# Output projection of a decoder layer: seven products of half-size blocks in place of eight

## The chip, the core and the metric

The kernel runs on one core of a Trainium2 chip. Its work goes to five engines, each with a queue of its own: TensorE (PE in the profile; the loading of stationary operands is shown apart as PEld), VectorE (DVE), ScalarE (ACT), GpSimd (POOL) and SyncE (SP), which issues DMAs. Each engine executes its instructions in the order in which they are written, and waits for other engines by semaphores. The metric is the time of one execution on the device in microseconds; lower is better.

## The reference

One layer on 512 tokens of width 1024, all in float32: a normalised input, one large input projection, two groups of heads (mLSTM and block-sparse attention), and an output projection into the residual. Only the end is changed:

```
y_ml = h_ml.reshape(B, S, ML_WIDTH) * jax.nn.silu(ml_z)     # 512 tokens x 512
y_at = o_at.reshape(B, S, AT_WIDTH) * jax.nn.silu(at_z)     # 512 tokens x 512
y = jnp.concatenate([y_ml, y_at], axis=-1).astype(x.dtype) @ w_out   # w_out 1024 x 1024
return x + y
```

In blocks, with two halves of 256 tokens (1 and 2), the two halves of the contraction (ml and at) and two halves of 512 output columns (0 and 1), each output block is a sum of two products: out(1,c) = y_ml1 B0c + y_at1 B1c, out(2,c) = y_ml2 B0c + y_at2 B1c. These are eight products of blocks, each 256 tokens by 512 by 512 columns.

## The kernel before

**Products.** TensorE multiplies in a rounded float32. To keep the precision, each operand is split into a rounded high part and the remainder (hi and lo), and each product is formed as three matmuls, hi by hi, hi by lo and lo by hi (`mm3`, L343). ScalarE makes the hi (a copy that rounds, CAST), VectorE the lo (the operand less its hi, TENSOR_TENSOR). So a weight piece of 128 x 1024 (two tiles of 128 rows by 512 columns) costs one CAST and one subtraction before it can be used.

**Weights** come in a list of pieces (L202 to L206 add the eight of w_out: `wo0` for columns 0 to 511, `wo1` for the others, four each). `load_w` (DMA at L234, into one of three buffers `raw`) loads a piece ahead of its use, `g_split` (L237) splits it into `whi` and `wlo`, and `need_w` waits for it.

**The order of the work.** Projections are one main stream that is written out in loops. All that runs beside them (splits, evacuations, heads) are small programs, held by `Plan`. After every few matmuls `plan.run()` resumes each program whose estimated time has come, and its instructions are appended to the queues of the engines. The estimates are clocks per engine with a rate and a fixed cost (`Engine`). The order in a queue is thus fixed when the kernel is built; at run time nothing overtakes. Instructions of VectorE, ScalarE and GpSimd are recorded at line L75, matmuls at L173, transposes at L177; the tile names tell them apart.

**Left sides.** `put_y` (L646) writes hi and lo of y for 128 features and all 512 tokens: the four mLSTM heads into buffers `br`, the four attention tiles (made in `ev_z`, L764, with the gate z in `cv0` and `cv1`) into `xh` and `xl`.

**The output stage** (L872 to L889). For the columns 0 to 511, four tiles of 128 tokens run in four PSUM banks at once, first over the mLSTM half of the contraction, then over the attention half. For the other columns the tiles run one by one, and the last one in two halves of 256 columns. `ev_out` (L863) adds the residual, loaded beforehand into `tq` and `tk`, on VectorE and stores the tile by a DMA of SyncE:

```
o = xres[half][t][:, c0:c1]
t_ = dve.tensor_tensor(o, ps[:, :c1 - c0], o, op=ALU.add)
banks.put(t_, ps)
nc.sync.dma_start(out[t * P:(t + 1) * P, half * 512 + c0:half * 512 + c1], o)
```

## Time and profile before

| | us |
|---|---|
| three runs | 310.49, 310.58, 310.62 (median 310.58) |
| the profiled execution, its span | 308.8 |
| median of the runs less that span | 1.8 |
| TensorE busy | 303.2 (98%) |
| VectorE busy | 185.8 (60%) |
| ScalarE busy | 150.2 (49%) |
| GpSimd busy | 58.3 (19%) |

The span reaches from the first to the last record of the profiled execution; the time of a run holds what lies around the records too. The busy times are shares of the whole span. The kernel moves 31.80 MB by DMA. A timeline's start is counted from the beginning of the span; equal instructions that follow each other are drawn together (x3), with the time from the first start to the last end.

### The profile page before, as it was taken

The numbers are of one execution on the slowest core, as the hardware profiler recorded it, in microseconds if no ns is written. First come the engines' busy times: TensorE is split into PE (matmuls) and PEld (weight loads), VectorE is DVE, ScalarE is ACT, GpSimd is POOL, SyncE is SP. The second block draws the span as 40 slices with busy tenths as digits, with TensorE's granted clock in tenths as the row PEclk, the third lists the DMA queues.
The fourth block names the chain that finished last, engine by engine and source line by source line (L and its number), as shares of the span: only waits on it lengthen the run. The fifth ranks groups of instructions, "written<-read, shape, count | busy, mean of one in ns | idle before, by whom it ended". The sixth has DMA issues, their size and how long they took to land.

```text
span 308.8 us, 4284 instructions
## 1 busy us (share of the span) xinstructions
PE 303.2 (98%) x1594; PEld 248.2 (80%) x1594; DVE 185.8 (60%) x395; ACT 150.2 (49%) x271; POOL 58.3 (19%) x94
## 2 busy tenths in 40 slices
PE   7999999999999999999999999999999999999995
PEld 3999888778888868886886888688889978788885
DVE  4892458935456549999627995501568999714111
ACT  3372754314365671775439356899763237420000
POOL 3000164262501800450150005110000060000000
PEclk9999999999999999999999999999999999999999
DMA  7997122141410410132103021400252102832101
GB/s 198 394 412 300 68 69 75 63 137 49 155 70 0 168 39 9 60 128 78 68 2 137 0 83 55 138 0 2 93 176 73 44 24 72 306 135 102 36 34 68
DMA packets 10821, 31.80 MB, mean 103 GB/s; under 512 B 1328, under 2 KB 1584, under 8 KB 10800
## 3 DMA queue, kind: packets, MB, share of 16 engines
q1 hardware_dynamic: 10800, 31.53, 28.8%
q8 instruction: 12, 0.20, 0.3%
q14 instruction: 9, 0.07, 0.1%
HBM read 29.42 MB, written 2.10 MB: 102 GB/s over the span
## 4 chain that ended last, share of the span: by engine, by line
PE 95%; DMA 2%; SPq 1%; DVE 1%; ACT 0%; issue 0%
PE bank L173 89%; PE bank L177 6%; DMA tq<-in_xT_dram 2%; ACT xh L75 0%; DVE wlo L75 0%; SPq L306 0%; DVE xl L75 0%; SPq L234 0%; SPq L232 0%; DVE tk L75 0%; SPq L230 0%; SPq L180 0%
## 5 line engine op out<-in xcount | busy, mean ns | idle before, releaser
L173 PE MATMUL bank<-whi,xh 128*128 128x512 f32 (+2 forms) x260 | 86.4, 367 | 0.7 <-DVE whi L75 0.7
L173 PE MATMUL bank<-wlo,xh 128*128 128x512 f32 (+2 forms) x260 | 85.1, 363 | 0.2 <-DVE wlo L75 0.2
L173 PE MATMUL bank<-whi,xl 128*128 128x512 f32 (+2 forms) x260 | 85.2, 363 | 0.0
L75 DVE TENSOR_TENSOR wlo<-raw,whi 128x1024 fp32r<-128x1024 f32 x39 | 48.0, 1241 | 10.8 <-ACT whi L75 9.2
L173 PEld LDWEIGHTS bank<-whi,xh 128*128 128x128 f32 x260 | 45.1, 188 | 8.7 <-ACT xh L75 1.1
L173 PEld LDWEIGHTS bank<-whi,xl 128*128 128x128 f32 x260 | 45.0, 188 | 8.1
L173 PEld LDWEIGHTS bank<-wlo,xh 128*128 128x128 f32 x260 | 45.1, 188 | 7.9 <-DVE wlo L75 0.6
L75 ACT CAST whi<-raw 128x1024 fp32r<-128x1024 f32 x39 | 40.8, 1048 | 19.8 <-PE bank L173 11.5
L173 PE MATMUL bank<-xh,whi 128*128 128x512 f32 x96 | 40.9, 426 | 0.0
L173 PE MATMUL bank<-xh,wlo 128*128 128x512 f32 x96 | 37.9, 395 | 0.0
L173 PE MATMUL bank<-xl,whi 128*128 128x512 f32 x96 | 37.7, 393 | 0.0
L75 POOL TENSOR_SCALAR b<-b,rec 128x128 f32<-128x128 f32 (+3 forms) x32 | 18.9, 612 | 84.6 <-DVE rec L75 67.1
L75 ACT ACTIVATE br<-bank,sm 64x512 fp32r<-64x512 f32 (+1 forms) x28 | 19.1, 684 | 14.7 <-DVE br L75 9.7
L173 PEld LDWEIGHTS bank<-xh,whi 128*128 128x128 f32 x96 | 18.2, 190 | 4.5 <-issue 2.1
L173 PE MATMUL bank<-whi,br 128*128 128x512 f32 (+1 forms) x72 | 21.4, 370 | 0.0
L173 PEld LDWEIGHTS bank<-xh,wlo 128*128 128x128 f32 x96 | 18.0, 188 | 4.2
L75 ACT ACTIVATE b<-b,mn 128x128 f32<-128x128 f32 (+3 forms) x32 | 17.6, 553 | 7.6 <-DVE mn L75 7.5
L173 PEld LDWEIGHTS bank<-xl,whi 128*128 128x128 f32 x96 | 18.2, 189 | 2.5
L75 DVE SCALAR_TENSOR_TENSOR br<-bank,sm,br 64x512 fp32r<-64x512 f32 (+1 forms) x20 | 15.0, 749 | 5.9 <-ACT br L75 5.6
L75 DVE CUSTOM_DVE_ANT_0 b<-bank,b 128x128 f32<-128x128 f32 (+3 forms) x32 | 14.2, 488 | 5.5 <-PE bank L173 5.4
L173 PEld LDWEIGHTS bank<-whi,br 128*128 128x128 f32 x72 | 13.1, 188 | 2.6
L177 PEld LDWEIGHTS bank<-ident,b 128*128 128x128 f32 (+1 forms) x104 | 12.3, 140 | 3.4 <-issue 0.4
(141 smaller groups left out, 374.1 us busy)
## 6 DMA issues: line engine op xcount, KB each, us to landing
raw<-in_w_in_dram SPq DMA_DIRECT2D x31, 512.0 KB, 3.2
raw<-in_w_out_dram SPq DMA_DIRECT2D x8, 512.0 KB, 3.5
b<-in_w_in_dram SPq DMA_DIRECT2D x3, 520.0 KB, 7.5
tq<-in_xT_dram SPq DMA_DIRECT2D x4, 256.0 KB, 5.4
tk<-in_xT_dram SPq DMA_DIRECT2D x4, 256.0 KB, 7.8
ot<-in_x_dram SPq DMA_DIRECT2D x2, 512.0 KB, 9.1
cv<-in_x_dram SPq DMA_DIRECT2D x2, 512.0 KB, 9.9
tq<-in_x_dram SPq DMA_DIRECT2D x4, 256.0 KB, 5.8
```

What stands on the lines that cost most here:

```text
L75: fn(out, *args, **kw)
L173: nc.tensor.matmul(out_, lhsT=lhsT, rhs=rhs, start=start, stop=stop, skip_group_check=True)
L177: nc.tensor.transpose(out_, in_, idn)
```

## The change

Eight products of blocks are replaced by seven, with an identity of the Strassen family. Its operands are sums and differences of blocks:

| product | left side, 256 tokens x 512 | weights, 512 x 512 |
|---|---|---|
| p5 | y_ml2 | B00 + B01 |
| p1 | xa = y_ml1 - y_at1 | B00 |
| p2 | y_at1 | B00 + B10 |
| p6 | r = y_ml2 - xa | p1's less p7's |
| p3 | c = y_ml1 - y_ml2 | B01 + B11 |
| p7 | e = r - y_at2 | B11 |
| p4 | y_at2 | B10 + B11 |

They are formed in this order. Each has two tiles of 128 tokens, four k-tiles of 128 and three matmuls of 512 columns: 24 matmuls. Products accumulate on each other in three pairs of PSUM banks (`CHAIN`): p5 and then p3 in one pair, p1, p6, p7 and p4 in another, p2 in its own. Between two products of a pair the sum so far is taken out, without the pair being given back, by `ev_prod`. After p5 and p1, ScalarE copies the two banks to SBUF (`vbuf` and `tk`), and a DMA issued by GpSimd adds the tile of x onto the copy (`accum_op`). After p2, p6, p3, p7 and p4, VectorE adds the bank to, or subtracts it from, the output block in SBUF. Where a block is complete it is stored by SyncE; the last tile is no longer halved.

The weights of p5, p2, p3 and p4 are loaded as two pieces onto each other: a plain DMA of SyncE, and 4.5 us later on the plan's clock an accumulating one of GpSimd (`g_load`). Those of p6 are a subtraction on VectorE. Loads go in the order p5, p1, p2, p7, p3, p4, into the three `raw` buffers and others that are free by then (`wraw`, such as `ot` and `sz`).

`put_ml` writes y_ml to `tq` and splits only the tokens of p5; the steps after the gates make xa and its split; `g_combos` makes the other left sides. `x_of(r, c, a)` is a tile of x in DRAM, `store` and `residual` are DMAs of SyncE, and `two`, `of` and `flat2` give views of a tile by k. The main stream then runs over the products:

```diff
@@ -191,29 +191,32 @@
...
+    PRODS = [("p5", [(0, 0), (0, 1)]), ("p1", [(0, 0)]), ("p2", [(0, 0), (1, 0)]), ("p6", []),
+             ("p3", [(0, 1), (1, 1)]), ("p7", [(1, 1)]), ("p4", [(1, 0), (1, 1)])]
+    for name, blocks in PRODS:
+        for u in range(2):
+            pieces.append((name, u, 512, w_out, [(c * 4 + 2 * r + u) * P * 1024 for r, c in blocks]))
     W = {}
+    NREG = sum(p[3] is w_in for p in pieces)
     raws = {}
+    nload, nsplit = [0], [0, sum(p[3] is w_in for p in pieces)]
+    def src_ap(i, b=0):
         _, _, n, src, o = pieces[i]
+        return bass.AP(tensor=src.tensor, offset=src.offset + o[b], ap=[[2 * n, P], [1, 2 * n]])
     def pair(t, n):
         return t[:, :2 * n].rearrange("p (k n) -> p k n", k=2)
@@ -232,19 +237,66 @@
-        raws[i] = pair(dst, n)
+        raws[i] = (dst, pair(dst, n))
     def g_split(i, copy=act.copy, parts=1):
         name, kk, n, _, _ = pieces[i]
-        raw = raws.pop(i)
+        if i >= NREG:
+            yield (0.0, lambda: i in raws and nsplit[1] >= i, False)
+        flat_raw, raw = raws[i][0], raws.pop(i)[1]
...
         W[name, kk] = (hi, lo)
+        if i >= NREG:
+            nsplit[1] = i + 1
+            if name == "p1":
+                wkeep["p1", kk] = flat_raw
+            else:
+                wraw.put(t_, flat_raw)
         load_w()
+    wraw = Bufs(plan, [])
+    nraw, lnext = [0], [0]
+    wkeep = {}
+    at = {(p[0], p[1]): i for i, p in enumerate(pieces)}
+    LOADS = [(n, u) for n in ("p5", "p1", "p2", "p7", "p3", "p4") for u in range(2)]
+    def raw_ok():
+        room = 3 - nraw[0] - max(0, NREG - nsplit[0])
+        return room > 0 or wraw.ok()
+    def raw_get():
+        if wraw.ok():
+            return wraw.get()
+        nraw[0] += 1
+        return wp.tile([P, 1024], F32, name="raw", tag="raw", bufs=3)
+    def g_load(j):
+        name, u = LOADS[j]
+        i = at[name, u]
+        yield (0.0, lambda: lnext[0] == j and raw_ok(), False)
+        dst = raw_get()
+        nc.sync.dma_start(dst, src_ap(i))
+        lnext[0] += 1
+        if len(pieces[i][4]) == 2:
+            yield plan.now + 4500.0
+            nc.gpsimd.dma_start(dst, src_ap(i, 1), accum_op=ALU.add)
+            yield plan.now + 5000.0
+        else:
+            yield plan.now + 5000.0
+        if name == "p7":
+            wkeep["p7", u] = dst
+            yield (0.0, lambda: ("p1", u) in wkeep and ("p6", u) not in wkeep, False)
+            d1 = wkeep["p1", u]
+            t_ = dve.tensor_tensor(d1, d1, dst, op=ALU.subtract)
+            wkeep["p6", u] = d1
+            yield t_
+            raws[at["p6", u]] = (d1, pair(d1, 512))
+        raws[i] = (dst, pair(dst, 512))
@@ -640,19 +692,34 @@
...
+    yml = tq
+    y_at = [cv[f // 2][:, f % 2] for f in range(4)]
+    X = {}
+    H = slice(0, 256), slice(256, 512)
+    def halves(t):
+        return t.rearrange("p (k n) -> p k n", n=256)
+    def put_ml(h, ps, scale, t_=0.0):
+        yield act.activation(yml[:, h], ps, AF.Copy, scale=scale)
+        hi, lo = X["p5"]
+        t_ = act.copy(hi(h), yml[:, h, H[1]])
         yield t_
+        yield dve.tensor_tensor(lo(h), yml[:, h, H[1]], hi(h).bitcast(F32), op=ALU.subtract)
...
@@ -755,7 +822,10 @@
...
         yield plan.now + SLACK
-        for t_ in put_y(h, ps, sm[:, C_MN + h:C_MN + h + 1]):
+        yield when(lambda: have["S"] == MLH)
+        if "p5" not in X:
+            X["p5"] = two([br.get() for _ in range(2)]), two([br.get() for _ in range(2)])
@@ -770,14 +840,70 @@
...
             t_ = dve.tensor_tensor(z, z, ot[:, f], op=ALU.mult)
-            yield when(lambda: have["proj"], t_)
-            for t_ in put_y(4 + f, z, None):
-                yield t_
+            yield when(lambda: have["y"] == MLH, t_)
+            if f == 0:
+                X["xa"] = b5.get()
+                X["p1"] = two([br.get() for _ in range(2)]), two([br.get() for _ in range(2)])
+            xa = halves(X["xa"][:, 0:1024])
+            x1 = xa[:, f]
+            yield dve.tensor_tensor(x1, yml[:, f, H[0]], z[:, H[0]], op=ALU.subtract)
+            hi, lo = X["p1"]
+            yield act.copy(hi(f), x1)
+            yield dve.tensor_tensor(lo(f), x1, hi(f).bitcast(F32), op=ALU.subtract)
+            have["p1"] += 1
         return ev
+    fl = lambda t: t.rearrange("p a n -> p (a n)")
+    def g_combos():
+        yield when(lambda: have["p1"] == 4)
+        wraw.put(plan.now, *[flat(ot)[:, 1024 * u:1024 * u + 1024] for u in range(2)])
+        xa = halves(X["xa"][:, 0:1024])
+        def plain(h, key):
+            for f in range(4):
+                yield act.copy(xh[:, f, H[h]], y_at[f][:, H[h]])
+                yield dve.tensor_tensor(xl[:, f, H[h]], y_at[f][:, H[h]], xh[:, f, H[h]].bitcast(F32), op=ALU.subtract)
+                have[key] += 1
+        for t_ in plain(0, "p2"):
+            yield t_
+        r, c, e = (b5.get()[:, 0:1024] for _ in range(3))
+        rv = halves(r)
+        yield when(lambda: step[0] >= 1)
+        yield dve.tensor_tensor(rv, yml[:, :, H[1]], xa, op=ALU.subtract)
+        yield act.copy(fl(xh[:, 4:6]), r)
+        dve.tensor_tensor(fl(xl[:, 4:6]), r, fl(xh[:, 4:6]).bitcast(F32), op=ALU.subtract)
+        X["p6"] = flat2(xh, 4), flat2(xl, 4)
+        have["p6"] = 4
+        yield when(lambda: step[0] >= 2)
+        yield dve.tensor_tensor(halves(c), yml[:, :, H[0]], yml[:, :, H[1]], op=ALU.subtract)
+        hi, lo = X["p3"] = X["p5"]
+        for k in range(4):
+            act.copy(hi(k), halves(c)[:, k])
+            t_ = dve.tensor_tensor(lo(k), halves(c)[:, k], hi(k).bitcast(F32), op=ALU.subtract)
+        yield t_
+        have["p3"] = 4
+        yield when(lambda: step[0] >= 3)
+        for u in range(2):
+            t_ = dve.tensor_tensor(halves(e)[:, 2 * u:2 * u + 2], rv[:, 2 * u:2 * u + 2], cv[u][:, :, H[1]], op=ALU.subtract)
+        yield t_
+        yield act.copy(fl(xh[:, 6:8]), e)
+        dve.tensor_tensor(fl(xl[:, 6:8]), e, fl(xh[:, 6:8]).bitcast(F32), op=ALU.subtract)
+        X["p7"] = flat2(xh, 6), flat2(xl, 6)
+        have["p7"] = 4
+        yield when(lambda: step[0] >= 4)
+        for t_ in plain(1, "p4"):
+            yield t_
+    step = [0]
...
@@ -841,52 +967,97 @@
...
+    for j in range(len(LOADS)):
+        plan.add(g_load(j), rank=1)
...
+    def ev_prod(ps, a, what, last, c0=0, c1=512):
+        t_ = plan.now
+        for r, c, op, end in what:
+            d = res[r, c, a][:, c0:c1]
+            if op is None:
+                yield act.copy(d, ps)
+                nc.gpsimd.dma_start(d, x_of(r, c, a), accum_op=ALU.add)
+                continue
+            t_ = dve.tensor_tensor(d, d, ps[:, :c1 - c0], op=op)
+            if end:
+                store(r, c, a, c0, c1)
+        if last:
             banks.put(t_, ps)
+        yield t_
+    ADD, SUB = ALU.add, ALU.subtract
+    bank = {}
+    CHAIN = {"p5": ("B", [(1, 1, None, False)]),
+             "p1": ("A", [(0, 0, None, False)]),
+             "p2": ("1", [(0, 0, ADD, True)]),
+             "p6": ("A", [(0, 1, SUB, False)]),
+             "p3": ("B", [(0, 1, ADD, True)]),
+             "p7": ("A", [(1, 1, SUB, True)]),
+             "p4": ("A", [(1, 0, ADD, True)])}
+    ends = {"p2", "p3", "p4"}
+    plan.add(g_combos(), rank=0.5)
+    for name, _ in PRODS:
+        key, what = CHAIN[name]
+        step[0] = [n for n, _ in PRODS].index(name)
+        first = (key, 0) not in bank
+        if first:
+            for a in range(2):
+                bank[key, a] = main_bank()
+        plan.until(lambda: name != "p1" or "p1" in X)
+        left = {"p1": X.get("p1"), "p2": (of(xh, 0), of(xl, 0)), "p4": (of(xh, 1), of(xl, 1))}
+        def part(ps, a, k, c0=0, c1=512, start=False, stop=False):
+            hi, lo = need_w(name, k // 2)
+            plan.until(lambda: name == "p5" or have[name] > k)
+            xs = left.get(name) or X[name]
+            ts = slice(a * P, (a + 1) * P)
+            mm3(ps, xs[0](k)[:, ts], xs[1](k)[:, ts], hi[:, k % 2, c0:c1], lo[:, k % 2, c0:c1], start, stop)
+        if name in ("p7", "p4"):
+            for a in range(2):
+                for k in range(4):
+                    part(bank[key, a], a, k, stop=k == 3)
+                    if a and k % 2 and name == "p7":
+                        split_w()
+                    plan.run()
+                plan.add(ev_prod(bank[key, a], a, what, name in ends), rank=0, ready=plan.now + SLACK)
+            continue
+        for k in range(4):
+            for a in range(2):
+                part(bank[key, a], a, k, start=first and k == 0, stop=k == 3)
                 plan.run()
+            if k % 2:
+                split_w()
+            if name in ("p1", "p2") and k == 0:
+                residual(*((0, 1) if name == "p1" else (1, 0)))
+        for a in range(2):
+            plan.add(ev_prod(bank[key, a], a, what, name in ends), rank=0, ready=plan.now + SLACK)
```

VectorE's queue before, in the output stage: the last split of a left side has just been written, and what follows are the lo parts of weights (`wlo`) and the additions that empty banks.

```order
L75 TENSOR_TENSOR wlo_2376<-raw_2145,whi_2375 128x1024
L75 TENSOR_TENSOR wlo_2379<-raw_2277,whi_2378 128x1024
L75 TENSOR_TENSOR tq_128<-bank5_91,tq_128 128x512
L75 TENSOR_TENSOR tq_128<-bank0_86,tq_128 128x512
L75 TENSOR_TENSOR tq_128<-bank4_90,tq_128 128x512
L75 TENSOR_TENSOR tq_128<-bank6_92,tq_128 128x512
L75 TENSOR_TENSOR wlo_2442<-raw_2299,whi_2441 128x1024
```

VectorE's queue in the changed kernel, from the end of p1 to p6's left side. `cv1` holds y_at, `b5_4` is r, `b5_3` is xa; `wlo_2399` is p2's second weight piece, `wlo_2419` and `wlo_2431` are p6's two, `wlo_2443` is p3's first; `bank3` and `bank7` are p2's banks.

```order
L75 TENSOR_TENSOR xl_112<-cv1_132,xh_111 128x256
L75 TENSOR_TENSOR wlo_2399<-sz_127,whi_2398 128x1024
L75 TENSOR_TENSOR xl_112<-cv1_132,xh_111 128x256
L75 TENSOR_TENSOR wlo_2419<-raw_1985,whi_2418 128x1024
L75 TENSOR_TENSOR b5_4_73<-tq_128,b5_3_72 128x1024
L75 TENSOR_TENSOR wlo_2431<-raw_1981,whi_2430 128x1024
L75 TENSOR_TENSOR tk_129<-tk_129,bank3_89 128x512
L75 TENSOR_TENSOR tk_129<-tk_129,bank7_93 128x512
L75 TENSOR_TENSOR wlo_2443<-ot_133,whi_2442 128x1024
L75 TENSOR_TENSOR xl_112<-b5_4_73,xh_111 128x1024
```

The left side of p6 (the last row) now stands behind two additions that need the end of p2 and behind a weight piece of p3.

Further on in the same queue, from p7's second weight piece (`wlo_2496`) and p4's first (`wlo_2519`) to p7's left side (`b5_0` is e); `bank1` and `bank4` hold p3.

```order
L75 TENSOR_TENSOR wlo_2496<-ot_133,whi_2495 128x1024
L75 TENSOR_TENSOR wlo_2519<-sz_127,whi_2518 128x1024
L75 TENSOR_TENSOR tk_129<-tk_129,bank1_87 128x512
L75 TENSOR_TENSOR tk_129<-tk_129,bank4_90 128x512
L75 TENSOR_TENSOR xl_112<-b5_0_69,xh_111 128x1024
```

Before, nothing but weight pieces and additions stood here; now the left side of the next product stands behind the two additions that need the end of the one before it.

ScalarE's queue before, at its end: the last gate, its hi, and weight pieces.

```order
L75 ACTIVATE cv1_132<-cv1_132 128x512
L75 CAST xh_111<-cv1_132 128x512
L75 CAST whi_2375<-raw_2145 128x1024
L75 CAST whi_2378<-raw_2277 128x1024
L75 CAST whi_2441<-raw_2299 128x1024
L75 CAST whi_2444<-raw_2391 128x1024
```

ScalarE's queue in the changed kernel, from the copies of p1's banks (`bank0`, `bank6`) to p6's left side: `xh` from `cv1` is p2's left side, `whi_2398` p2's second weight piece, `whi_2418` and `whi_2430` p6's two, `whi_2442` p3's first.

```order
L75 COPY tk_129<-bank0_86 128x512
L75 COPY tk_129<-bank6_92 128x512
L75 CAST xh_111<-cv1_132 128x256
L75 CAST whi_2398<-sz_127 128x1024
L75 CAST xh_111<-cv1_132 128x256
L75 CAST whi_2418<-raw_1985 128x1024
L75 CAST whi_2430<-raw_1981 128x1024
L75 CAST whi_2442<-ot_133 128x1024
L75 CAST xh_111<-b5_4_73 128x1024
```

The copies that empty p1's banks, which were no work of ScalarE's before, stand ahead of the second half of p2's operands and of all of p6's.

## Rows read from the trace of the kernel before

**Rows 1.** The page: span, busy times, and shares of the chain that ended last.

```profile
span 308.8 us, 4284 instructions
...
PE 303.2 (98%) x1594; PEld 248.2 (80%) x1594; DVE 185.8 (60%) x395; ACT 150.2 (49%) x271; POOL 58.3 (19%) x94
...
PE 95%; DMA 2%; SPq 1%; DVE 1%; ACT 0%; issue 0%
```

**Rows 2.** Timeline: start, length, engine; first and last matmul of the output stage, last addition.

```profile
260.51 0.39 PE L173 MATMUL bank<-whi,br 128*128 128x512 f32 x1
...
305.04 0.28 PE L173 MATMUL bank<-whi,xl 128*128 128x256 f32 x1
305.35 0.42 DVE L75 TENSOR_TENSOR tk<-bank,tk 128x256 f32<-128x256 f32 x1 [2.42 <-PE bank L173]
```

**Rows 3.** Windows: length, busy PE PEld DVE ACT POOL (count), PE clock, DMA.

```profile
240.00:260.50 20.50, 20.50 (x114) 17.24 (x114) 19.91 (x59) 9.43 (x15) 5.24 (x8) 1.00 0.12 30
260.50:271.60 11.10, 11.10 (x49) 8.87 (x48) 7.63 (x10) 4.49 (x6) 0.00 (x0) 1.00 0.85 309
271.60:282.80 11.20, 11.20 (x50) 9.15 (x49) 2.08 (x3) 1.12 (x2) 0.00 (x0) 1.00 0.23 86
305.40:308.80 3.40, 0.00 (x0) 0.00 (x0) 0.38 (x1) 0.00 (x0) 0.00 (x0) 0.92 0.11 39
```

**Rows 4.** Groups of instructions, 260.4 to 309: count, busy us, mean ns, idle before.

```profile
L173 PE MATMUL bank<-whi,br 128*128 128x512 f32 x56 | 18.3, 396 | 0.0
...
L173 PE MATMUL bank<-whi,br 128*128 128x256 f32 x16 | 3.2, 282 | 0.0
```

**Rows 5.** VectorE from 260: timeline, then groups of its additions.

```profile
260.19 1.22 DVE L75 TENSOR_TENSOR wlo<-raw,whi 128x1024 fp32r<-128x1024 f32 x1
...
262.58 1.89 DVE L75 TENSOR_TENSOR xl<-cv,xh 128x512 fp32r<-128x512 f32 x3
...
266.70 2.36 DVE L75 TENSOR_TENSOR wlo<-raw,whi 128x1024 fp32r<-128x1024 f32 x2 [0.26 <-ACT whi L75]
...
L75 DVE TENSOR_TENSOR tk<-bank,tk 128x512 f32<-128x512 f32 x3 | 2.1, 692 | 12.3 <-PE bank L173 12.3
...
L75 DVE TENSOR_TENSOR tk<-bank,tk 128x256 f32<-128x256 f32 x2 | 0.8, 425 | 4.6 <-PE bank L173 4.6
```

**Rows 6.** ScalarE from 259: timeline, then a group of copies from PSUM.

```profile
259.20 1.65 ACT L75 CAST xh<-cv 128x512 fp32r<-128x512 f32 x3
...
265.11 0.62 ACT L75 CAST xh<-cv 128x512 fp32r<-128x512 f32 x1 [1.77 <-DVE cv L75]
...
265.63 1.99 ACT L75 CAST whi<-raw 128x1024 fp32r<-128x1024 f32 x2
...
270.62 1.05 ACT L75 CAST whi<-raw 128x1024 fp32r<-128x1024 f32 x1 [2.99 <-issue]
...
L75 ACT COPY b<-bank 128x256 f32<-128x256 f32 x8 | 3.0, 375 | 2.9 <-PE bank L177 2.9
```

**Rows 7.** Timeline ahead of the stage: weight loads, a gate, GpSimd's next work.

```profile
221.62 40.15 SPq L234 DMA_DIRECT2D raw<-in_w_out_dram  x7
...
235.86 0.63 ACT L75 ACTIVATE cv<-cv 128x512 f32<-128x512 f32 x1 [2.87 <-DVE cv L75]
...
246.66 0.20 POOL L75 TENSOR_SCALAR mst<-mst 128x4 f32<-128x4 f32 x1 [39.66 <-DVE mst L75]
246.94 1.03 POOL L75 TENSOR_TENSOR mst<-mst,mhalf 128x4 f32<-128x4 f32 x1
```

**Rows 8.** DMA issues with us to landing; SyncE's time per issue, min/median/max ns.

```profile
tk<-in_x_dram SPq DMA_DIRECT2D x4, 256.0 KB, 6.8
...
out_dram<-tk SPq DMA_DIRECT2D x3, 256.0 KB, 2.0
out_dram<-tk SPq DMA_DIRECT2D x2, 128.0 KB, 1.9
...
L868 SPq DMA_DIRECT2D out_dram<-tk x5: 332/332/333, 289.3 to 305.8; - x5
```

More of the change, by code (lines that the diff above doesn't have):

```diff
@@ L199, in hybrid_layer @@
         for kk in range(4):
-            pieces.append((name, kk, n, w_in, off))
+            pieces.append((name, kk, n, w_in, [off]))
             off += P * 2 * n
-    off = 0
-    for half in range(2):
-        for kk in range(4):
-            pieces.append((f"wo{half}", kk, 512, w_out, off))
-            off += P * 2 * 512
+    PRODS = [("p5", [(0, 0), (0, 1)]), ("p1", [(0, 0)]), ("p2", [(0, 0), (1, 0)]), ("p6", []),
[3 more added lines that the diff above has]
+            pieces.append((name, u, 512, w_out, [(c * 4 + 2 * r + u) * P * 1024 for r, c in blocks]))
     xh = sb("xh", [P, KT, S], F32R)
@@ L641, in hybrid_layer, with two, of, flat2 @@
     have["silu"] = have["sig"] = have["gates"] = have["mlive"] = have["W"] = have["S"] = have["y"] = 0
-    yh, yl = {}, {}
-    def put_y(f, src, scale, t_=0.0):
-        hi, lo = (br.get(), br.get()) if f < 4 else (xh[:, f - 4], xl[:, f - 4])
-        if scale is None:
-            yield act.copy(hi, src)
-            t_ = dve.tensor_tensor(lo, src, hi.bitcast(F32), op=ALU.subtract)
-        else:
-            yield act.activation(hi, src, AF.Copy, scale=scale)
-            t_ = dve.scalar_tensor_tensor(lo, src, scale, hi.bitcast(F32), op0=ALU.mult, op1=ALU.subtract)
-        yh[f], yl[f] = hi, lo
-        yield t_
+    yml = tq
[8 more added lines that the diff above has]
+        t_ = act.copy(hi(h), yml[:, h, H[1]])
+        yield t_
+        yield dve.tensor_tensor(lo(h), yml[:, h, H[1]], hi(h).bitcast(F32), op=ALU.subtract)
+    def two(tiles):
+        v = [halves(t) for t in tiles]
+        return lambda k: v[k // 2][:, k % 2]
+    def of(t, h):
+        return lambda k: t[:, k, H[h]]
+    def flat2(t, k0):
+        v = halves(t[:, k0:k0 + 2].rearrange("p a n -> p (a n)"))
+        return lambda k: v[:, k]
     def g_mlstm(h):
@@ L757, in g_mlstm @@
         yield plan.now + SLACK
-        for t_ in put_y(h, ps, sm[:, C_MN + h:C_MN + h + 1]):
+        yield when(lambda: have["S"] == MLH)
+        if "p5" not in X:
+            X["p5"] = two([br.get() for _ in range(2)]), two([br.get() for _ in range(2)])
+        for t_ in put_ml(h, ps, sm[:, C_MN + h:C_MN + h + 1]):
             yield t_
@@ L778, in hybrid_layer @@
+    step = [0]
     have["proj"] = 0
+    for name in ("p1", "p2", "p3", "p4", "p6", "p7"):
+        have[name] = 0
     psz = [[banks.get() for _ in range(2)] for _ in range(NT)]
@@ L846, in hybrid_layer @@
     have["proj"] = 1
-    def out_mm(ps, half, t, k, c0=0, c1=512):
-        plan.until(lambda: k in yh)
-        hi, lo = need_w(f"wo{half}", k // 2)
-        ts = slice(t * P, (t + 1) * P)
-        mm3(ps[:, :c1 - c0], yh[k][:, ts], yl[k][:, ts], hi[:, k % 2, c0:c1], lo[:, k % 2, c0:c1],
-            k == 0, k == KT - 1)
-    xres = []
-    plan.until(lambda: have["y"] == MLH)
-    for half in range(2):
-        r = tk if half else tq
-        for t in range(NT):
-            nc.sync.dma_start(r[:, t], x[t * P:(t + 1) * P, half * 512:half * 512 + 512])
-        xres.append([r[:, t] for t in range(NT)])
@@ L863, in ev_out @@
-    def ev_out(half, t, c0=0, c1=512):
-        def ev(ps):
-            o = xres[half][t][:, c0:c1]
-            t_ = dve.tensor_tensor(o, ps[:, :c1 - c0], o, op=ALU.add)
-            banks.put(t_, ps)
-            nc.sync.dma_start(out[t * P:(t + 1) * P, half * 512 + c0:half * 512 + c1], o)
-            yield t_
-        return ev
-    ps4 = [main_bank() for _ in range(NT)]
-    for ks in ((0, 1, 2, 3), (4, 5, 6, 7)):
-        for t in range(NT):
-            for k in ks:
-                out_mm(ps4[t], 0, t, k)
-                plan.run()
-        for _ in range(2):
-            split_w()
@@ L880, in hybrid_layer @@
-    for t in range(NT):
-        plan.add(ev_out(0, t)(ps4[t]), rank=0, ready=plan.now + SLACK)
-    for t in range(NT):
-        cols = ((0, 512),) if t < NT - 1 else ((0, 256), (256, 512))
-        for c0, c1 in cols:
-            ps = main_bank()
-            for k in range(KT):
-                out_mm(ps, 1, t, k, c0, c1)
-                plan.run()
-            plan.add(ev_out(1, t, c0, c1)(ps), rank=0, ready=plan.now + SLACK)
+    plan.until(lambda: have["y"] == MLH)
+    for t in (flat(sz), vbuf):
+        wraw.put(plan.now, t[:, 0:1024])
@@ new lines, in hybrid_layer, with x_of, residual @@
+    res = {}
+    room = [tk[:, t] for t in range(NT)] + [sz[:, 2 + u] for u in range(2)] + [vbuf[:, 1024 + 512 * u:1536 + 512 * u] for u in range(2)]
+    for r in range(2):
+        for c in range(2):
+            for a in range(2):
+                res[r, c, a] = room.pop(0)
+    def x_of(r, c, a):
+        t = 2 * r + a
+        return x[t * P:(t + 1) * P, c * 512:c * 512 + 512]
+    def residual(r, c):
+        for a in range(2):
+            nc.sync.dma_start(res[r, c, a], x_of(r, c, a))
@@ new lines, in store @@
+    def store(r, c, a, c0=0, c1=512):
+        t = 2 * r + a
+        nc.sync.dma_start(out[t * P:(t + 1) * P, c * 512 + c0:c * 512 + c1], res[r, c, a][:, c0:c1])
+    def ev_prod(ps, a, what, last, c0=0, c1=512):
[10 more added lines that the diff above has]
+        if last:
+            banks.put(t_, ps)
+        yield t_
```

9 lines of the change are left out of this document (5 added, 4 removed).

## Prediction

> **What bounds the kernel now.** The page comes first. TensorE (PE) is busy for 303.2 of 308.8 us, and the chain of work that ended last is 95% PE [rows 1]. So a microsecond counts only if it is taken from PE's queue or added to it as a gap. The timeline then places the changed part: the output projection's first matmul starts at 260.51 and its last at 305.04, with an end near 305.16; after it come one VectorE addition and a store [rows 2]. Read by stages, PE has no gap there, while VectorE works 7.63 us of the first 11.1 and 2.08 of the next 11.2, and ScalarE 4.49 and 1.12 [rows 3]. That is the slack that the change will spend.
>
> **What the change removes.** The stage has 56 matmuls of 512 and 16 of 256 columns with one pair of operands, and half as many with each of four other pairs [rows 4]: 168 and 48, the work of 192 of 512. 44.65 us over 192 gives 0.2326 us each. Seven products of 24 matmuls are 168, so PE loses 24 x 0.2326 = **5.58 us**, and one product lasts 5.58. The DMA that feeds this is not what PE waits for now, so the smaller or larger traffic counts only where it makes an operand late.
>
> **What it adds on VectorE and ScalarE.** Weights: 14 pieces are split where 8 were (ScalarE copy 128x1024, VectorE subtraction 128x1024), and two more subtractions make the weights of p6. Left sides: each of five products needs a combination and its own split; p5 and p1 take theirs from heads and gates that the old kernel also split. Prices: two subtractions of 1024 take 2.36 and one takes 1.22, so the second starts 1.14 behind the first; three of 512 take 1.89 against 0.69 for one, 0.60 apart; one of 256 takes 0.425, so some 0.33 apart [rows 5]. On ScalarE two copies of 1024 take 1.99 against 1.05, 0.94 apart; three of 512 take 1.65 against 0.62, 0.51 apart; one of 256 from PSUM takes 0.375, some 0.30 apart [rows 6]. Both engines have room for the sum. What counts is the order, since each engine takes its instructions in the order in which they are written.
>
> **Until the end of p1 nothing waits.** The stretch before 260.5 has PE full and VectorE at 19.91 of 20.5 us [rows 3], so a delay there would show. The old kernel splits a weight piece before the heads' last steps, the new one a little later, and the halves of y that it splits are shorter, so I take 0. The first accumulating DMA (p5) follows a plain load that is issued at 221.62, as the first load of output weights is now. Even if that takes 6.8 us it is there at 228.4, GpSimd, which issues the accumulation, is idle until 246.66, and the ScalarE copy that needs it stands ahead of a step that ran at 235.86 [rows 7, 8]: 7.4 us are left. p1's left side follows the last gate by some 4 us of VectorE and ScalarE work at these prices, and p5 covers 5.58.
>
> **Where p6 waits.** p1 ends at 260.5 + 2 x 5.58 = 271.7. ScalarE's two copies of p1's banks stand ahead of everything that p2's second half and p6 need, so they hold ScalarE back until then (the order rows show it). From 271.9: copy to 272.4, xh to 272.7, the split of p2's second piece done 273.75, xh, p6's pieces done 275.0 and 275.9, p3's first piece done 276.9. VectorE follows: xl 272.8, lo of p2's second piece 273.8 to 275.05, xl, lo of p6's first piece at 275.3, p6's left combination 276.45 to 277.65, lo of p6's second piece at 277.6. p2 wanted its second piece's lo at 274.7: a wait of **0.35**, and p2 ends at 277.6. Then VectorE takes the two additions that empty p2 (278.7, 279.3), the lo of p3's first piece (279.9), and only then p6's left lo (281.05, done 282.3). PE wants p6's left hi at 277.6; its ScalarE copy can start at 277.65 and is done at 278.75: a wait of 1.2. Two matmuls later it wants the left lo: from 279.25 to 282.3, a wait of 3.05. Together **4.25** at p6.
>
> **Where p7 waits.** p6 resumes at 282.3 with 22 matmuls left (5.1) and p3 adds 5.58, to 293.0. VectorE has both banks of p3 to empty before p7's left lo. The second bank is complete 0.2 after p3's end, its addition takes 0.6, the lo 1.24: done 295.05. PE wants it two matmuls into p7, at 293.5: **1.6**. p4's material is ready earlier. The waits add up to 6.2.
>
> **The tail.** The old kernel halves its last tile: the addition takes 0.425 on 256 columns and a 128 KB store lands in 1.9. The new one ends with 512 columns: 0.69, and 256 KB in 2.0 [rows 5, 8]. That adds **0.37**.
>
> **The accumulating DMAs.** No row of this case shows one, nor any DMA that GpSimd issues. From both sides: the shortest landing of 256 KB is the 2.0 of a store, the longest the 6.8 of loads that queue behind six others [rows 8]. GpSimd's time per issue lies between SP's 0.33 and GpSimd's own longest row in this stretch, 1.03 [rows 7, 8]. The tightest one is the second addition of x onto p1's result: it can be issued at 272.5 to 274.6 and VectorE wants it at 279.3, so it has 4.7 to 6.8 us. I take some 4 us, nearer to the store, since only a few transfers are in flight there, so it costs nothing. At 6.8 and the slow issue it costs 2 to 3. [...]
>
> **Sum.** -5.58 + 0.35 + 4.25 + 1.6 + 0.37 = +0.99 us. The profiled execution spans 308.8 and would span 309.8. The median of the runs shown, 310.58, lies 1.8 above that span, and I carry the same 1.8 over: **311.6 us**. The identity's gain is real, but it comes back as waits behind VectorE's queue.
>
> **Rivals.** Faster: VectorE is not behind when p2 ends. Then only the fixed queue is left at p6 (bank complete 0.2, addition 0.6, lo 1.14, left lo 1.24, less the two matmuls of 0.47: 2.7) and 1.6 at p7, and -5.58 + 4.3 + 0.37 = -0.9 gives 309.7. The point is whether the lo of p6's second piece is done by 277.6; I have it at 278.8, so 1.2 us of the seven operations would have to be missing. For it speaks only the roundness of my spacings. 0.13. With no wait at all it would be 305.4: 0.02, since the order of the instructions excludes it.
>
> Slower by the clock: the granted clock is 1.00 while PE works and 0.92 in the mean of the 3.4 us after the last matmul [rows 3]. [...] 0.25. [...]
>
> Slower by late DMAs: the additions of x, or the piece for p3, land after VectorE or ScalarE wants them, at the prices above, 312.6 to 314.6. They stand ahead of p6's left side in both queues, so p6 pays for all of it. 0.15.
>
> **How the numbers follow.** Forecast case 0.45, by itself 310.9 to 312.3; faster rival 0.15 in all; clock 0.25; late DMAs 0.15. A difference under 0.2% (0.6 us) can't be told from none. The faster rival lies below 309.96, so faster 0.15. Of the forecast case the part under 311.2 is some 0.4 of it: same 0.20. The rest, slower 0.65. The range 309.5 to 314.8 leaves out the tail of the clock case and the case without waits.
>
> **What would show it.** In the profile after: 24 fewer matmul equivalents in the output stage; PE gaps before p6 put down to ScalarE's xh and then VectorE's xl, of 1.2 and 3.05; one of 1.6 before p7, put down to xl; the granted clock at 1.00 through p6; ScalarE idle before the copy of p1's bank. It is wrong if PE's waits sum to under 5 or over 7.5, if a wait is put down to a DMA of GpSimd's, if PE waits before 271, or if the clock falls.

## The result: 3.7% slower

The changed kernel takes 321.75 us in the median of four runs (321.35 to 323.46), the kernel before 310.53. The ratio is 1.037, with a 95% interval of 1.034 to 1.040. The profiled execution spans 319.7 us where before it was 308.8 [rows 1], 10.9 us more.

The page after: span, busy time of each engine, and the shares of the chain that ended last.

```profile
span 319.7 us, 4286 instructions
...
PE 300.8 (94%) x1546; PEld 243.5 (76%) x1546; DVE 204.9 (64%) x426; ACT 164.7 (52%) x299; POOL 68.8 (22%) x106
...
PE 85%; DMA 8%; DVE 4%; issue 1%; SPq 1%; ACT 1%; POOLq 0%; DVEq 0%
```

PE has 48 matmuls fewer (24 of 512 columns, and the 48 halves are now 24 whole ones), but its share of the chain fell from 95% to 85%, and DMA and VectorE stand in it. By windows, in the columns of [rows 3] (the last two are the DMA share and the GB/s):

```profile
260.50:271.60 11.10, 11.10 (x49) 8.90 (x48) 8.72 (x17) 5.03 (x11) 3.46 (x4) 1.00 0.90 264
271.60:282.80 11.20, 6.95 (x28) 4.72 (x26) 5.95 (x7) 6.36 (x9) 2.94 (x4) 1.00 1.09 270
282.80:290.20 7.40, 0.00 (x0) 0.00 (x0) 3.09 (x5) 1.99 (x2) 1.39 (x2) 0.51 1.07 244
290.20:293.30 3.10, 3.05 (x7) 2.47 (x8) 3.10 (x5) 1.94 (x5) 0.00 (x0) 0.51 0.82 202
293.30:304.00 10.70, 9.70 (x42) 7.51 (x40) 8.60 (x12) 4.62 (x8) 0.00 (x0) 1.00 0.06 21
```

Until 271.6 PE is full. From 282.8 to 290.2 it does nothing, and the granted clock is 0.51 of full speed; in the next 3.1 us it is busy at 0.51 too, 7 matmuls where 13 would fit. The DMA share is 0.90 in the first window and 1.07 to 1.09 from there to 290.2: full. What PE waited for, and then what VectorE waited for, from 240 on (total us, times, longest):

```profile
PE bank L173 <- DVE xl L75: 9.4, 2, 8.0
PE bank L173 <- ACT xh L75: 3.5, 1, 3.5
PE bank L173 <- DVE wlo L75: 0.2, 1, 0.2
...
DVE tk L75 <- DMA tk<-in_x_dram: 7.7, 2, 4.3
```

The timeline of GpSimd, ScalarE, VectorE and PE around the gap shows who is late:

```profile
272.22 0.86 POOL L1005 DMA_DIRECT2D tk<-in_x_dram  x1 [1.58 <-ACT tk L75]
274.63 1.21 POOL L1005 DMA_DIRECT2D tk<-in_x_dram  x1
...
279.50 1.04 ACT L75 CAST whi<-ot 128x1024 fp32r<-128x1024 f32 x1 [3.42 <-DMA ot<-in_w_out_dram]
280.45 1.04 ACT L75 CAST xh<-b 128x1024 fp32r<-128x1024 f32 x1
...
282.24 0.69 DVE L75 TENSOR_TENSOR tk<-tk,bank 128x512 f32<-128x512 f32 x1 [3.36 <-DMA tk<-in_x_dram]
287.24 0.69 DVE L75 TENSOR_TENSOR tk<-tk,bank 128x512 f32<-128x512 f32 x1 [4.31 <-DMA tk<-in_x_dram]
287.84 1.22 DVE L75 TENSOR_TENSOR wlo<-ot,whi 128x1024 fp32r<-128x1024 f32 x1
288.97 1.22 DVE L75 TENSOR_TENSOR xl<-b,xh 128x1024 fp32r<-128x1024 f32 x1
...
290.25 0.79 PE L173 MATMUL bank<-whi,xl 128*128 128x512 f32 x1 [7.98 <-DVE xl L75]
```

GpSimd issues the two additions of x onto p1's copy at 272.2 and 274.6. VectorE can empty p2's banks only at 282.24 and 287.24, 10.0 and 12.6 us later, and p6's left side (`xl<-b`) stands behind these two and a weight piece. On ScalarE p6's hi (`xh<-b`) stands behind a weight piece of p3 that landed late too.

The DMA queues from 256 to 288 (packets, MB, share of the time of the 16 engines), and DMA issues with the median us from issue to landing:

```profile
q0 software_dynamic: 1200, 3.34, 56.1%
q1 hardware_dynamic: 1686, 4.92, 42.7%
...
ot<-in_w_out_dram POOLq DMA_DIRECT2D x1, 512.0 KB, 9.7
tk<-in_x_dram POOLq DMA_DIRECT2D x2, 256.0 KB, 11.2
```

q0 holds GpSimd's accumulating transfers, q1 the plain ones. 56.1% of 32 us is 18.0 us for 3.34 MB, 186 GB/s; 42.7% is 13.7 us for 4.92 MB, 360 GB/s. Together they fill 31.6 of 32 us.

### The profile page after: what moved, and what is told of

It reads as the page before. It is cut to its first block, busy times and chain, and to the rows that moved or that the text cites. A ratio compares the mean times of both kernels' runs of the same rounds, so it can differ in the third digit from the quotient of the medians.

```text
span 319.7 us, 4286 instructions
## 1 busy us (share of the span) xinstructions
PE 300.8 (94%) x1546; PEld 243.5 (76%) x1546; DVE 204.9 (64%) x426; ACT 164.7 (52%) x299; POOL 68.8 (22%) x106
## 4 chain that ended last, share of the span: by engine, by line
PE 85%; DMA 8%; DVE 4%; issue 1%; SPq 1%; ACT 1%; POOLq 0%; DVEq 0%
PE bank L173 79%; DMA raw<-in_w_out_dram 6%; PE bank L177 5%; DMA tq<-in_xT_dram 2%; DVE wlo L75 1%; DVE xl L75 1%; DVE br L75 1%; ACT xh L75 0%; DVE b L75 0%; DVE cv L75 0%; ACT whi L75 0%; SPq L358 0%; DVE tk L75 0%; DVE sz L75 0%; SPq L239 0%
## 5 line engine op out<-in xcount | busy, mean ns | idle before, releaser
L75 DVE TENSOR_TENSOR wlo<-raw,whi 128x1024 fp32r<-128x1024 f32 x40 | 49.1, 1234 | 10.5 <-ACT whi L75 8.9
L75 ACT CAST whi<-raw 128x1024 fp32r<-128x1024 f32 x40 | 41.8, 1048 | 20.5 <-PE bank L173 11.5
L75 ACT ACTIVATE br<-bank,sm 64x512 fp32r<-64x512 f32 x24 | 16.4, 683 | 11.8 <-DVE br L75 9.7
L75 ACT ACTIVATE b<-b,mn 128x128 f32<-128x128 f32 (+3 forms) x32 | 17.6, 553 | 7.5 <-DVE mn L75 7.4
L75 DVE SCALAR_TENSOR_TENSOR br<-bank,sm,br 64x512 fp32r<-64x512 f32 x16 | 12.0, 749 | 5.9 <-ACT br L75 5.6
L173 PE MATMUL bank<-whi,br 128*128 128x512 f32 x48 | 15.4, 396 | 0.0
L177 PE MATMUL bank<-ident,b 128*128 128x128 f32 (+1 forms) x104 | 14.7, 268 | 0.0
```

The lines of the kernel that those rows point to most:

```text
L75: fn(out, *args, **kw)
L173: nc.tensor.matmul(out_, lhsT=lhsT, rhs=rhs, start=start, stop=stop, skip_group_check=True)
L177: nc.tensor.transpose(out_, in_, idn)
```

## The experiments

**e1: without the additions of x.** In `ev_prod`:

```diff
                 yield act.copy(d, ps)
-                nc.gpsimd.dma_start(d, x_of(r, c, a), accum_op=ALU.add)
                 continue
```

> The four accumulating DMAs that add tiles of x onto the copies of p5 and p1 are left out, so two of the four output blocks lack their residual; all else stands as in the changed kernel. Theory L (the late additions of x onto p1 hold VectorE, and VectorE's queue holds p6's left side): the 7.7 us that VectorE waited for them go, p6's two waits fall from 11.5 us to some 4 to 5, the clock stays up, and the time falls from 321.75 to 312 to 314. Rival S (the DMA engines are simply full from 256 to 288, so p6 and p3 lack their weights too): taking away 1 of 8.3 MB moves the other landings by some 5 us at most, the wait only changes its name to weight pieces, and the time stays above 317. Rival V (VectorE's own queue, as forecast, is the cost): nothing changes by more than 1 us.

314.82 us (314.13 to 315.28), ratio 1.012 (1.010 to 1.014): 6.9 us of the 11.2 are gone. What PE waited for, and the windows around p6:

```profile
PE bank L173 <- DVE xl L75: 4.2, 2, 2.7
PE bank L173 <- ACT xh L75: 0.9, 1, 0.9
PE bank L173 <- DVE wlo L75: 0.2, 1, 0.2
```

```profile
271.60:282.70 11.10, 7.30 (x30) 4.97 (x28) 8.88 (x11) 8.61 (x11) 1.71 (x2) 0.97 0.98 284
282.70:288.80 6.10, 6.08 (x14) 4.79 (x15) 4.72 (x7) 3.32 (x6) 0.85 (x1) 0.50 0.98 179
```

Neither PE nor VectorE waits for what a DMA of x held up any more; ScalarE still waits 1.5 us in all for weights of p3. The additions of x are what cost the 6.9, as theory L says, and rivals S and V are out. But "the clock stays up" was wrong: 14 matmuls ran at a granted clock of 0.50, in 6.1 us where 3.3 would do, and so the time is above the range.

**e2: the second weight loads without accumulating.** In `g_load`:

```diff
-            nc.gpsimd.dma_start(dst, src_ap(i, 1), accum_op=ALU.add)
+            nc.gpsimd.dma_start(dst, src_ap(i, 1))
```

> The second loads of the weights of p5, p2, p3 and p4 stay where they are, in GpSimd's queue and with the same bytes, but overwrite instead of accumulating, so the weights of these products are not sums. The x additions still accumulate. Theory A (an accumulating transfer holds the DMA engines about twice as long per byte: 186 against 360 GB/s while its packets run): some 8 us of DMA engine time leave the stretch from 256 to 288, the additions of x land in 5 to 8 us instead of 10 to 12.5, and the time falls to 314 to 317. Rival B (it is bytes or GpSimd's way of issuing): the same bytes by the same way take as long, and the time stays within 1 us of 321.75.

318.70 us (316.99 to 320.04), 3.05 us faster: between both theories. With the same bytes the additions of x still landed in 8.4 us (median), and VectorE waited 4.9 us for them instead of 7.7. Accumulating weights are a part of the delay. The rest remains with the same bytes in flight and with the additions of x, which still accumulate; this run does not divide it between the two.

**e3: x loaded plain, added on VectorE.**

```diff
-                yield act.copy(d, ps)
-                nc.gpsimd.dma_start(d, x_of(r, c, a), accum_op=ALU.add)
+                t_ = dve.tensor_tensor(d, d, ps[:, :c1 - c0], op=ALU.add)
...
+            if name == "p5" and k == 0:
+                residual(1, 1)
+                residual(0, 0)
```

> All of the computation is kept. The tiles of x for the blocks of p5 and p1 are loaded by SyncE at the start of p5, plain, and VectorE adds the bank to them, where ScalarE copied the bank and a DMA of GpSimd added x. Theory L: nothing of p6 waits for a late addition of x any more, which saves about what the first run saves; VectorE gets four additions of 0.69 us, which stand in its queue ahead of operands and cost 1 to 3 us of it. 313 to 316. Rival S: the stretch from 256 to 288 has the same bytes, 1 MB of it cheaper, and the weights are late instead: 317 to 320.

314.64 us (313.89 to 314.85), as theory L has it, but the waits that are left are those of rival S. What PE waited for, then ScalarE:

```profile
PE bank L173 <- ACT xh L75: 5.3, 1, 5.3
...
ACT whi L75 <- DMA raw<-in_w_out_dram: 3.5, 1, 3.5
ACT whi L75 <- DMA ot<-in_w_out_dram: 2.5, 1, 2.5
```

p6's hi stands behind p3's weights on ScalarE, and these land late, as they did in the changed kernel. So rival S was right on the place, but not on the time.

**e4: the transfers by themselves,** behind the last store of the kernel before, with a VectorE copy of one column as the sign that a transfer has landed (`after`):

```diff
+    after(o1[:, 0:1], v1[:, 0:1])
+    nc.gpsimd.dma_start(v1, piece(2), accum_op=ALU.add)
+    after(v1[:, 0:1], c1_[:, 0:1])
+    nc.gpsimd.dma_start(c1_[:, 0:512], x[0:P, 0:512], accum_op=ALU.add)
```

> The kernel before, with transfers added behind its last store, one after the other and with nothing else in flight: 512 KB plain by SyncE, 512 KB plain by GpSimd, 512 KB accumulating by GpSimd, 256 KB of x accumulating by GpSimd; then two accumulating of 512 KB and a plain one of 512 KB together. What is left out of the computation: nothing. Theory A (accumulating costs DMA engine time): plain by GpSimd lands like plain by SyncE plus its issue, some 3.5 us; accumulating 512 KB takes 5 to 5.6, and 256 KB 3 to 3.5; the three together take 8 to 9 to the last one. Rival G (the way through GpSimd is what is slow): plain by GpSimd takes over 5 us too. Rival F (a fixed latency, no occupation): the three together land as soon as one alone.

```profile
306.75 0.38 SPq L910 DMA_DIRECT2D sz<-in_w_out_dram  x1
310.51 0.15 DVE L901 COPY seen<-sz 128x1 f32<-128x1 f32 x1 [3.85 <-DMA sz<-in_w_out_dram]
...
311.18 0.79 POOL L912 DMA_DIRECT2D ot<-in_w_out_dram  x1 [56.73 <-DVE ot L902]
314.99 0.15 DVE L901 COPY seen<-ot 128x1 f32<-128x1 f32 x1 [4.14 <-DMA ot<-in_w_out_dram]
...
315.93 0.90 POOL L914 DMA_DIRECT2D vbuf<-in_w_out_dram  x1 [3.97 <-DVE vbuf L902]
321.54 0.15 DVE L901 COPY seen<-vbuf 128x1 f32<-128x1 f32 x1 [6.20 <-DMA vbuf<-in_w_out_dram]
```

Plain, 512 KB take 3.8 us by SyncE and 3.8 by GpSimd: the way through GpSimd costs nothing here. Accumulating, they take 5.6 (and 256 KB of x 3.85). Two accumulating and a plain one together were complete 10.3 us after the first issue. So an accumulating transfer occupies the engines, it doesn't only come late: theory A, with a sum somewhat above its 8 to 9. By its packets, the accumulating 512 KB alone fills the 16 engines for 50.7% of the 6.5 us from 315.5 to 322, 3.3 us, and the plain one by GpSimd for 17.6% of the 9 us from 306 to 315, 1.6 us. In the changed kernel the two rates differ by 360 / 186 = 1.94; no run here shows the cause.

**e5: the order alone.** In `g_combos` the steps from `rv` to `have["p6"]` become a program of their own that is added after two of p2's four features (and no longer waits for p1 to begin), and the additions that empty p2's and p3's banks are written later:

```diff
+        for n, t_ in enumerate(plain(0, "p2")):
+            yield t_
+            if n == RAFTER:
+                plan.add(left_r(), rank=0.7)
...
+    LATE = {'p2': 5000.0, 'p3': 4000.0}
...
-            plan.add(ev_prod(bank[key, a], a, what, name in ends), rank=0, ready=plan.now + SLACK)
+            plan.add(ev_prod(bank[key, a], a, what, name in ends), rank=0, ready=plan.now + SLACK + LATE.get(name, 0.0))
```

> All of the computation and every DMA of the changed kernel are kept; only the order in VectorE's and ScalarE's queues changes: p6's left side is made after half of p2's, the additions that empty p2's banks are written some 5 us later and those of p3 some 4 us later. Theory Q (a late addition of x costs only because p6's left side, and p7's behind p3, stand behind it in VectorE's queue): the additions of x land as late as before (10 to 12 us), but PE waits 1 to 4 us in place of 13.1, and the time is 308 to 312.5. Rival S (the DMA engines are full and every product lacks its operands): p3's weights are late in any order, PE waits over 6 us, and the time is above 314.

309.30 us (309.18 to 309.81), ratio to before 0.997 (0.995 to 0.998), 12.4 us below the changed kernel. The additions of x onto p1's copy, with the median us to landing, and what PE waited for:

```profile
tk<-in_x_dram POOLq DMA_DIRECT2D x2, 256.0 KB, 10.9
```

```profile
PE bank L173 <- DVE wlo L75: 1.4, 3, 0.8
PE bank L173 <- DVE xl L75: 0.6, 1, 0.6
```

The additions of x are as late as in the changed kernel, and neither PE nor VectorE waits for them any more. Theory Q holds. The 2.0 us that PE still waits are for other operands; ScalarE waits 8.2 us in all for weights that land late.

**e6, e7 and e8: the sums on GpSimd.** `g_load` loads one block for p2, p3 and p4, and GpSimd adds the raw tile of p1 (for p2) or of p7 (for p3 and p4) in place of the accumulating DMA (p6's weights, which overwrite p1's tile, wait until p2's sum is formed):

```diff
+        if name in SUMS:
...
+            t_ = pool.tensor_tensor(dst, dst, held[SUMS[name], u], op=ALU.add)
```

e7 has the order of e5 besides, with p1's copies 2 us later; e8 is e6 with 18 more matmuls.

> All of the computation is kept. The second blocks of p2, p3 and p4 are not loaded: GpSimd adds the raw weights of p1 (for p2) and of p7 (for p3 and p4), which still lie in SBUF, to the one block that is loaded. Six accumulating transfers of 512 KB go; the four of x stay; the order of VectorE's queue is that of the changed kernel. Theory A (accumulating traffic fills the DMA engines): the additions of x land in 5 to 7 us, nothing waits for a DMA, PE keeps about the waits that were forecast for VectorE's order (1 to 1.5 at p6's hi, 3 to 4 at its lo), the clock falls in them as in the first run, and the time is 311 to 314.5. Rival: GpSimd's additions of 128x1024 take longer than 3 us or slow VectorE, the sums come late, and the time stays above 315.

> All of the computation is kept. The sums on GpSimd as in the run above, and the left side of p6 early and the additions that empty p1, p2 and p3 later, as in the first run of this call. If the cost is late transfers times VectorE's order and nothing else, no wait of PE's is left, the clock stays at 1.00, 24 matmuls are saved, and the time is 305 to 306.5, some 5 us below the kernel before. If a bound of another kind was hidden behind the waits (PSUM banks, the load on VectorE, the clock), it is 308 or more.

> The sums on GpSimd with the order unchanged, as in the second run of this call, and 18 matmuls of 512 columns into a bank that nobody reads: 5 ahead of p6's first matmul and 13 ahead of its third, where PE waits for the left side. [...]

323.45 us (323.39 to 323.49), 317.03 (316.85 to 317.78) and 323.81 (322.54 to 325.41). In e6 the additions of x landed in 4.1 and 5.9 us (medians, onto p1's and p5's copy), as theory A had it or sooner, and still the kernel was slower: the times of theory A in e6 and of e7's first case were missed by 9 and 10.5 us, and the rival of e6 came. GpSimd and VectorE in e6:

```profile
253.85 2.45 POOL L75 TENSOR_TENSOR raw<-raw 128x1024 f32<-128x1024 f32 x1
...
270.35 8.59 POOL L75 TENSOR_TENSOR ot<-ot,vbuf 128x1024 f32<-128x1024 f32 x1
...
280.05 8.68 DVE L75 TENSOR_TENSOR wlo<-ot,whi 128x1024 fp32r<-128x1024 f32 x1 [3.37 <-ACT whi L75]
```

An addition that takes GpSimd 2.45 us took 8.59 while VectorE worked without a break, and then a subtraction of VectorE's that takes 1.22 took 8.68 while GpSimd had three additions. In e7 the same addition of GpSimd's took 10.8 us, and a VectorE one 6.5; PE waited 5.8 behind them, through ScalarE. e8 asks what the clock's fall in the gaps costs, and says little about it: one gap, of 3.3 us, lay in p2, ahead of the added matmuls, and p6's hi came 4.3 us after the first five of them.

**e12: the two engines by themselves,** behind the last store of the kernel before:

```diff
+    nc.gpsimd.tensor_tensor(c1_, c1_, o1, op=ALU.add)
+    for _ in range(4):
+        nc.vector.tensor_tensor(s2, s1, o2, op=ALU.add)
```

> The kernel before, with instructions added behind its last store: four additions of 128x1024 on VectorE alone; one on GpSimd alone; one on GpSimd with four on VectorE at the same time; one on GpSimd with four copies on ScalarE. What is left out of the computation: nothing. Theory X (GpSimd's additions and VectorE's exclude each other): alone 4.6 and 2.4 us; together GpSimd's takes 2.4 us plus the 4.6 of VectorE's, or VectorE's first one takes 2.4 us more; with ScalarE beside it, 2.4. Rival: together each takes as long as alone, and the 8.6 us of e6 were a wait for something else.

```profile
306.71 5.00 DVE L909 TENSOR_TENSOR sz<-sz,ot 128x1024 f32<-128x1024 f32 x4
...
312.26 2.34 POOL L914 TENSOR_TENSOR vbuf<-vbuf 128x1024 f32<-128x1024 f32 x1 [57.78 <-DVE vbuf L899]
...
314.89 7.01 DVE L909 TENSOR_TENSOR sz<-sz,ot 128x1024 f32<-128x1024 f32 x4
315.12 3.19 POOL L916 TENSOR_TENSOR cv<-cv,ot 128x1024 f32<-128x1024 f32 x1 [0.52 <-DVE cv L899]
...
321.93 4.28 ACT L921 COPY sz<-sz 128x1024 f32<-128x1024 f32 x4 [46.72 <-DVE sz L909]
322.30 2.35 POOL L919 TENSOR_TENSOR cv<-cv,ot 128x1024 f32<-128x1024 f32 x1 [3.99 <-DVE cv L899]
```

Alone 5.00 and 2.34 us; together VectorE takes 7.01, nearly their sum, and GpSimd 3.19; beside ScalarE GpSimd takes 2.35. So the two engines' additions hold each other up, as theory X has it: VectorE's four took 2.0 us longer than alone, where its second case has 2.4. GpSimd's addition took 0.85 us longer than alone, less than one of VectorE's additions (5.00 / 4 = 1.25); why one took 8.59 us in e6, no run shows.

**e9: the order, and x behind the weights.** e5, with p1's copies written 2 us later, the plain loads of the other tiles of x moved from the first k-tile of p1 and p2 to the third of p2 and p3, and the additions of x behind p3's accumulating loads in GpSimd's queue:

```diff
+    XWHEN = (lambda: ("p3", 1) in accd), (lambda: ("p3", 1) in accd and step[0] >= 4)
...
                 yield act.copy(d, ps)
+                yield (0.0, XWHEN[r], False)
                 nc.gpsimd.dma_start(d, x_of(r, c, a), accum_op=ALU.add)
```

> All of the computation is kept, with the same number and size of DMAs as the changed kernel. The order of e5, the copies of p1's banks some 2 us later in ScalarE's queue, and the four additions of x behind the accumulating loads of p3's weights in GpSimd's queue (those of p5's block behind p4's begin); the plain loads of the other tiles of x two steps later. If what was left in e5 is that p3's and p4's weights stand in the DMA queue behind additions of x that nobody needs yet, PE's waits fall from 2.0 to under 0.5 us and the time from 309.3 to 306.5 to 308. If the engines are full with bytes whatever the order, p3's second piece is still late and the time stays at 309 to 309.5.

**306.86 us** (306.59 to 306.96), ratio to before 0.988 (0.987 to 0.990): the full computation, the same 24 matmuls saved, the same DMAs in number and size, and 1.2% faster than the kernel before. The largest move is that of the additions of x onto p5's copy, which are issued at 285.92 in place of 266.67; those onto p1's stay at 272.2, but both of p3's accumulating loads are now ahead of them. (`step[0] >= 4` is the start of p3, not of p4 as the expectation has it.) Several things were moved at once, and no run divides the 2.4 us to e5 among them. The time is in the forecast range; PE's waits fell to 1.2, not under 0.5. One wait of PE's is left, and the clock stays at 1.00 in all four windows from 260.5 to 301. The first and the last matmul of the stage, what PE waited for, and the window with the wait:

```profile
260.58 0.39 PE L173 MATMUL bank<-whi,br 128*128 128x512 f32 x1
...
300.80 0.40 PE L173 MATMUL bank<-whi,xl 128*128 128x512 f32 x1
```

```profile
PE bank L173 <- DVE xl L75: 1.2, 1, 1.2
```

```profile
282.80:294.00 11.20, 10.01 (x44) 7.79 (x43) 10.44 (x14) 5.03 (x8) 2.65 (x3) 1.00 1.01 234
```

VectorE is busy 10.44 of 11.2 us there, so it is the likely limit now; e13 tries that.

**e13: p2's banks emptied later still.** In e9:

```diff
-    LATE = {'p1': 2000.0, 'p2': 5000.0, 'p3': 4000.0}
+    LATE = {'p1': 2000.0, 'p2': 9000.0, 'p3': 4000.0}
```

> The kernel of e9 with one number changed: the additions that empty p2's banks are written 9 us after the end of p2 on the plan's clock instead of 5, which puts the two of them (0.6 us each) behind p7's left side in VectorE's queue. All of the computation is kept. If the 1.2 us that PE still waited for that left side are VectorE's backlog and nothing else, they go, and the time falls from 306.9 to 305.5 to 306.2. If the wait is a weight piece that lands late, it stays, under another name, and the time stays within 0.5 us of 306.9.

307.54 us (307.40 to 308.25): the wait for p7's left side fell from 1.2 to 0.4, but PE waited 1.0 for the addition that empties p7's first bank, and that addition had waited 0.7 for a late addition of x. The total of PE's waits is 1.7. Neither case of the expectation came: the backlog was one part, and a late transfer took its place.

**e10: e1 with the gaps filled.** In `part`, for p6's first product: 4 matmuls ahead of the first and 11 ahead of the third,

```diff
+                for n in range(11):
+                    mm(spare, xh[:, 0, 0:P], xh[:, 0])
```

> The kernel of e1 (the additions of x onto p5's and p1's copies left out), and 15 matmuls of 512 columns into a bank that nobody reads: 4 ahead of p6's first matmul and 11 ahead of its third, where PE waits 0.9 and 2.7 us for the left side. [...]

The run asks whether e1's 14 matmuls at a granted clock of 0.50 cost time of their own. They did: 310.14 us (309.79 to 310.33), 4.7 below e1. The windows that answer to those of e1:

```profile
277.50:282.70 5.20, 4.99 (x21) 3.45 (x20) 5.20 (x7) 2.62 (x3) 0.95 (x2) 1.00 0.90 326
282.70:288.80 6.10, 6.10 (x28) 4.98 (x27) 6.10 (x11) 3.91 (x7) 0.76 (x1) 1.00 0.97 173
```

28 matmuls in the 6.1 us in which e1 had 14, at a granted clock of 1.00. From the first of e1's 14 to the matmul behind them it took 6.14 us, where 14 x 0.233 is 3.26: the clock cost e1 2.9 us. The rest of the 4.7 is not the clock: the plan counts the added matmuls in its time, and by that wrote p7's left side ahead of the additions that empty p3's banks, so e1's 1.5 us of wait at p7 went as well. In e10 VectorE makes that left side at 289.38 and empties p3's banks at 293.12; in e1 the banks come first, at 295.81, and the left side at 297.12.

## Why the prediction was wrong

**The saving** was right. In e9 the first matmul of the stage starts at 260.58 and the last at 300.80. Less the 1.2 us of wait and some 0.25 us until the matmuls follow each other at their old distance again, 38.8 us are left for 167 steps, 0.232 each, as before.

**Until the end of p1 nothing waits:** right; the first wait of the stage is 0.2 us in p2, of the 0.35 that were forecast.

**The waits of VectorE's order** were right in place and cause, and nearly in size: with the late transfers gone (e1) they are 0.2, 0.9, 2.7 and 1.5, where 0.35, 1.2, 3.05 and 1.6 were forecast.

**The accumulating DMAs are the step that failed.** "I take some 4 us, nearer to the store, since only a few transfers are in flight there, so it costs nothing": they took 10.0 and 12.6, well beyond the upper bound of 6.8. So the term of the sum that was put at nothing cost 6.9 us (e1), more than twice the 2 to 3 that it gave for the slow case, and PE's waits at p6 were 3.5 and 8.0 instead of 0.9 and 2.7. I looked at the one transfer and its nearest row, and never added up what is in flight with it. From 256 to 288 twelve transfers of 512 KB and ten of 256 KB are issued, 8.9 MB. The old kernel's rows would have told most of what that means: 309 GB/s at a DMA share of 0.85 [rows 3] is 364 GB/s when full, so even plain they need some 24 us of the 32. That the 3.7 MB that accumulate take twice as long per byte no row of before could tell; with it the estimate is some 35 us, and the engines are full for all of the 32. How little room there is, e2 shows: with plain loads in place of the accumulating ones of the weights only 3.05 us come back. The old kernel's stage moved 309 GB/s for 11 us and then 86. A landing time out of a busy stretch (6.8, behind six others) was an estimate for a queue of seven, not an upper bound. Of the some 10 us by which the forecast was too low, 6.9 go with the additions of x, and 3.2 are left in e1, most of it the clock.

**The rivals.** "Slower by late DMAs" named the place ("p6 pays for all of it") but at 2 to 3 us. "Slower by the clock" came too: the granted clock was 0.51 from 282.8 to 293.3, and the 7 matmuls from 290.25 to 293.33 took 3.08 us instead of 1.63, so 1.45. No row and no run shows the price of the clock case, on which the upper end of the range, 314.8, rests; the runs showed a clock of 0.51 with 7 matmuls here and of 0.50 with 14 in e1, at 0.44 us each instead of 0.233. I treated the two as alternatives; the late transfer made the gap that the clock fell in. The two matmuls between the waits, at 281.55 and 281.88, didn't hold the clock up: it was 0.50 from 284 to 288. Even e1's gaps of 0.9 and 2.7 cost 2.9 (e10). The forecast case itself, then, was 2.9 too low: e1 measures it without late transfers and takes 314.8, not 311.6, and e10, with the gaps filled, 310.1.

**The sum by its own terms:** -5.6, waits 13.1 and some 0.95 until the matmuls follow each other again behind four of them, the clock 1.45, and 0.64 more from the end of the last matmul's step to the end of the span (0.37 forecast): 10.6 of the 10.9 us between the spans. The stage also starts 0.1 later; 0.2 is left open.

**Its own signs** told it: waits of 13.1 us (over 7.5), VectorE's wait for a DMA of GpSimd's ahead of p6, and the clock's fall.

**Slips in the working** that change nothing: only p6, p3 and p7 need a combination, not five products; 2 to 3 us on 311.6 begin at 313.6, not at 312.6; an even spread from 310.9 to 312.3 has 0.2 of its length under 311.2, not 0.4.

So the loss comes neither from the identity nor from accumulating by itself, but from late transfers together with an order in which the next product's operand stands behind them: e5 keeps every transfer as late as it was and is faster than the kernel before.
